# Attention's banks as two tiles, gate columns turned on VectorE and stored as rows, four pairs of modulations added in one bank each

## The chip, the cores and the metric

The kernel runs on one NeuronCore of one Trainium2 chip. The core has a matrix engine (TensorE, PE in the profile), three other compute engines (VectorE or DVE, ScalarE or ACT, GpSimd or POOL), a sync engine (SP) that issues transfers, and 16 DMA engines. Each engine runs its own queue in order and waits on semaphores of the others. TensorE writes only to PSUM, 8 banks of 512 float32 values in each of 128 partitions. The metric is the device time of one execution in microseconds (us); times before and after are compared by medians of several runs.

## What is computed

One layer of a hybrid block on 512 latent tokens with 256 context tokens, D_MODEL = 2048, all in float32. The parts that the change touches are the modulation vectors and the gate (first and last lines) and attention.

```python
shift, scale, gate = jnp.split(silu_c @ w_ada[l] + b_ada[l], 3, axis=-1)
shift_c, scale_c, gate_c = jnp.split(silu_cc @ w_ada[l] + b_ada[l], 3, axis=-1)
h = _modulate(_rmsnorm(xs, norm_g[l]), shift[:, None], scale[:, None])
hc = _modulate(_rmsnorm(cs, norm_g[l]), shift_c, scale_c)
...
p = h @ w_l
q = _rope(_rmsnorm(_heads(p, OFF_Q, N_Q_HEADS), q_norm_g[l]), cos, sin) * q_scale
...
attn = _attention(q, jnp.concatenate([k, kc], axis=1), jnp.concatenate([v, vc], axis=1))
y = _merge(p[..., OFF_ZA:], attn, w_proj_a[l], w_proj_b[l], w_out[l])
new_xs = xs + gate[:, None] * y
```

`_merge` multiplies attention and a Fourier mix with SiLU gates, projects both, weighs them with sigmoid gates and applies the output projection; the output is a final RMSNorm.

## The kernel before

Large products are made in three passes on split operands (`mm3`, lines 339 to 341): each float32 operand is split into a rounded part and its remainder (`split_from`, line 181 on ScalarE, line 182 on VectorE), and high x high, high x low and low x high are added in PSUM. Most weight products use a two by two block scheme with seven products (`Group`, P1 to Q4).

The start (to about 130 us) makes the modulations and the first projection. The columns of `x` are walked in 16 blocks of 128 channels (`KK = 16`). For one block `kb`, `modulate(kb)` takes a bank (`bank2`, tag `pd` in the profile), runs 16 matrix-vector products (`matvec`, line 567; the profile has two records for each) with the block's shift and scale weights as the moving operand, and copies the 128 x 256 result to SBUF on ScalarE (`taken`, line 583). The stationary operand is `c2`: for each of 16 row blocks, 32 columns, of which the first two hold silu of the two conditioning vectors and the rest zeros. Four row blocks run in the four column strips of the array, so the result has four groups of 32 rows, with the sums in the first two rows of each. `turned(kb)` turns the copy with two transposes (line 588) into the other half of the same bank, `factors(kb)` adds the four groups on VectorE (line 599) and makes the columns `gain` and `shift` (lines 600 and 602), and `make_h` applies them to `x`. Blocks 6 to 13 go in four pairs (the loop at line 844): both matrix-vector runs, each followed by its copy and the loads of the block two further on (line 477), some other matmuls (`some`), the transposes of both, then `factors` and `make_h` for each. In this part the orders of TensorE, ScalarE and VectorE are those of the text (`manual_schedule`); later a scheduler orders the engines by priority.

From about 150 to 803 us eight weight groups run (two-bank tiles `x` and `y` from the pool `psp`, tags x, y0 and y1). The last product of the last group sums into `x` tiles; at its end ScalarE copies one (line 1160) and VectorE reads another (line 1089). Then attention's pool `psq` is opened (line 1461): one tile `banks` of eight banks, of which the views `banks[0]` are the first six and `banks[1]` the last two. The six hold four score and transpose areas of 768 columns (`wide`); of the two, one is the accumulator of the filler (a branch projection that is interleaved with attention), the other serves values and query transposes. `reuse_waits="tile"` makes a new tile's first user wait for the users of the older tiles that lay in its place. TensorE starts attention with two filler steps of three matmuls each (line 1496), then the scores of step 0.

The gate vector is made on VectorE: 32 products with row sums (line 1369) leave two halves for each of 16 blocks in `gparts`, 128 partitions x 32 columns. After attention (lines 1744 to 1746) the halves and the bias are added into `gcol` (128 x 16), and GpSimd's queue stores it to `gs` in DRAM as 16 rows of 128, that is, turned by the access pattern of the store. `load_rows` (line 1783) reads `gs` as rows, broadcast to all partitions, about 100 us later. GpSimd's queue also issues the accumulating loads of the seven-product scheme (line 292) and the gate loads (line 1636).

Of the kernel before, what the change touches and what calls it, by code (L numbers as in the profile page):

```python
# [10 lines left out]
F32 = mybir.dt.float32  # L11
F32R = mybir.dt.float32r
ACT = mybir.ActivationFunctionType
ALU = mybir.AluOpType
AX = mybir.AxisListType
# [3 lines left out]
P = 128  # L19
# [3 lines left out]
KK = D // P  # L23
# [100 lines left out]
def block_kernel(ctx, tc, xT, ctx_rows, ctx_toks, x, c_row, w_ss, w_gate, vecs, qkg, rope, dft_c, dft_s,  # L124
                 w_start, w_g, w_pab, w_o, final_g, out):
    nc = tc.nc
# [6 lines left out]
    const = sb("const")  # L133
# [9 lines left out]
    gs = dsc.tile([KK, P], F32, name="gs")  # L143
# [13 lines left out]
    def uid(s):  # L157
        cnt[0] += 1
        return f"{s}{cnt[0]}"
# [14 lines left out]
    def bank2():  # L174
        return ps.tile([P, 512], F32, tag="b2", bufs=2, name=uid("pd"))
# [179 lines left out]
    cvt, bada, ng = small[:, : 2 * KK], small[:, 2 * KK : 5 * KK], small[:, 5 * KK :]  # L355
# [1 line left out]
    nc.vector.tensor_scalar(bsc1, bada[:, KK : 2 * KK], 1.0, None, op0=ALU.add)  # L357
    shift = const.tile([P, KK, 2], F32, name="shift")
    gain = const.tile([P, KK, 2], F32, name="gain")
    gcol = const.tile([P, KK], F32, name="gcol")  # L360
    gparts = const.tile([P, 2 * KK], F32, name="gparts")

    pairs = []
# [58 lines left out]
    for g in range(LAST + 1):  # L422
        for name in ONE_GROUP:
            if (g, name) == (LAST, "Q4"):
                stream_keys(0)
            if g == KV:
                f = CTX_FORMS.index(next(f for n, f, _, _ in PRODUCTS if n == name))
                stream(("cf", name), cf_d[:, :, f].rearrange("i p j c -> p i j c"), 1024, 8, dst=ctx_tiles)
            stream_product(name, g, w_g[g], BY_DVE_GATES if g else ())
            for pc in range(4):  # L430
                p = context_piece(g, name, pc)
# [36 lines left out]
    pa, pap = region("pa", "right")  # L468
# [16 lines left out]
    def load_start():  # L485

        may[0] = 1
        with tc.issue_after(last_load[0]):
            load_more()
        assert not may[0]  # L490
        last_load[0] = asked[0].ins

    def wada_load(kb):
        r = []
        for h in range(2):
            r.append(pap.tile([P, 8, 256], F32, tag="wada", bufs=4, name=uid("wa")))
            for k in (0, 4) if (kb, h) == (0, 1) else (0,):
                n = 4 if (kb, h) == (0, 1) else 8
                ask(nc.sync, r[-1][:, k : k + n, :], w_ss[kb, :, 8 * h + k : 8 * h + k + n, :])
        return r  # L500
# [3 lines left out]
    wada = {0: wada_load(0)}  # L504
# [2 lines left out]
    wada[1] = wada_load(1)  # L507
    load_start()

    c2 = pap.tile([P, KK, 32], F32, name="c2")  # L510
    nc.vector.memset(c2, 0.0)
    rt = pap.tile([P, 1], F32, name="rt")
    ce = pap.tile([P, 2 * KK], F32, name="ce")
    with tc.issue_after(nc.scalar.activation(ce, cvt, ACT.Exp, scale=-1.0).ins):
        nc.scalar.activation(rt, ones[:, 0:1], ACT.Sqrt)
    nc.vector.tensor_scalar(ce, ce, 1.0, None, op0=ALU.add)
    nc.vector.reciprocal(ce, ce)
    nc.vector.tensor_tensor(c2[:, :, 0:2].rearrange("p k j -> p j k"),
                            cvt.rearrange("p (j k) -> p j k", j=2),
                            ce.rearrange("p (j k) -> p j k", j=2), op=ALU.mult)  # L520
    fch = ppool.tile([P, 2, 2 * P], F32R, name="fch")
# [38 lines left out]
            nc.tensor.matmul(acc[:, t * P : t * P + P], pick[:, t, :], r, start=True, stop=True)  # L560
        return acc

    def matvec(kb, h):
        acc, w = two[kb][:, :256], wada[kb][h]
        for k in range(8):
            j, n = k % 4, 8 * h + k
            nc.tensor.matmul(acc[32 * j : 32 * j + 32], c2[:, n, :], w[:, k, :], start=n < 4, stop=n >= KK - 4)

    o_of, sp_of = {}, {}

    two = {}

    def modulate(kb, meanwhile=lambda: None):
        two[kb] = bank2()
        for h in range(2):
            matvec(kb, h)
        meanwhile()
        return taken(kb)

    def taken(kb):  # L580
        o = o_of[kb] = pap.tile([P, 256], F32, tag="ada_o", bufs=2, name=uid("ado"))
        wada.pop(kb)
        return nc.scalar.copy(o, two[kb][:, :256])

    def turned(kb):
        o = o_of.pop(kb)
        for i in range(2):
            nc.tensor.transpose(two[kb][:, 256 + P * i : 256 + P * i + P], o[:, P * i : P * i + P], ident)
        if kb == 0:
            warm(3, o)  # L590

    def columns(kb):
        turned(kb)
        factors(kb)

    def factors(kb):
        sp = two.pop(kb)[:, 256:]
        r = pap.tile([P, 2, 2], F32, tag="ada_r", bufs=2, name=uid("adr"))
        nc.vector.tensor_reduce(r, sp.rearrange("p (h g r) -> p h r g", h=2, g=4)[:, :, 0:2, :], axis=AX.X, op=ALU.add)
        nc.vector.tensor_scalar(gain[:, kb, :], r[:, 1, :], bsc1[:, kb : kb + 1], ng[:, kb : kb + 1],  # L600
                                op0=ALU.add, op1=ALU.mult)
        last = nc.vector.tensor_scalar(shift[:, kb, :], r[:, 0, :], bada[:, kb : kb + 1], None, op0=ALU.add)
        return last
# [173 lines left out]
    with tc.manual_schedule(engines={E.PE}):  # L777
        warm(8, ones)
        norms = token_norms()
        two[0] = bank2()  # L780
        matvec(0, 0)
        rx0.append(spread(*norms))
        matvec(0, 1)
        with tc.manual_schedule(engines={E.Activation, E.DVE}):
            nc.scalar.copy(rx, rx0[0])
            by_root(0)
            split_next()
            taken(0)
            wada[2] = wada_load(2)
            load_start()  # L790
            columns(0)
            row_hi(0)
            scaled(0)
            row_lo(0)
            split_next()
            by_root(1)
            some(4)
            modulate(1)
            rest = split_hi()
            wada[3] = wada_load(3)  # L800
            load_start()
            some(1)
            columns(1)
            some(1)
            row_hi(1)
            rest()
            scaled(1)
            row_lo(1)
            some(2)
            for kb in range(1, 4):  # L810
                k = kb + 1
                some(2 + (kb == 1))
                by_root(k)
                modulate(k, split_next)
                if kb < 3:
                    wada[k + 2] = wada_load(k + 2)
                    load_start()
                hold()
                some(2 - (kb == 1))
                columns(k)  # L820
                row_hi(k)
                release()
                scaled(k)
                if kb < 3:
                    some(2)
                row_lo(k)
                if kb == 3:
                    some(2)
                    by_root(5)
                    modulate(5)  # L830
                    for k in (6, 7):
                        wada[k] = wada_load(k)
                        load_start()
                    hold()
                    some(2)
                    columns(5)
                    row_hi(5)
                    release()
                    scaled(5)
                    load_rope()  # L840
                    row_lo(5)
                else:
                    some(2)
            for kb in range(4, KK - 4, 2):
                some(3)
                split_next()
                some(5)
                split_next()
                if kb == 6:
                    rotations()  # L850
                k = kb + 2
                for i in range(2):
                    modulate(k + i)
                    if k + 2 + i < KK:
                        wada[k + 2 + i] = wada_load(k + 2 + i)
                        for _ in range(2 if k + 2 + i == KK - 3 else 1):
                            load_start()
                some(1)
                for i in range(2):
                    turned(k + i)  # L860
                factors(k)
                make_h(k, lambda: some(1))
                factors(k + 1)
                make_h(k + 1, lambda: some(1))
                if k >= 8:
                    form_row(k - 8)
                    form_row(k - 7)
                some(1)
                if kb == KK - 6:
                    split_table(0)  # L870
                    split_from(get(("dftc", 0)), fch[:, 0, :], fch[:, 1, :])
                    load_start()
            for k in (KK - 2, KK - 1):
                some(2 if k < KK - 1 else 3)
                modulate(k)
                some(1)
                columns(k)
                make_h(k)
                split_next()
                if k < KK - 1:  # L880
                    load_start()
                form_row(k - 8)
        some(1)
        some(8)
# [95 lines left out]
    banks = []  # L980
# [478 lines left out]

    pgs.close()  # L1460
    psq = ctx.enter_context(tc.tile_pool(name="psq", bufs=1, space=PSUM, reuse_waits="tile"))
    whole_psum = psq.tile([P, 8, 512], F32, name="banks")
    banks += [whole_psum[:, :6, :], whole_psum[:, 6:, :]]
    last_y[:] = [0, 0]
    wide = [flat(banks[0])[:, NKEY * i : NKEY * i + NKEY] for i in range(4)]
    fill_acc, b1 = banks[1][:, 0, :], lambda: banks[1][:, 1, :]
# [219 lines left out]
    for i in range(NSTEP + 3):  # L1686
        h, t = divmod(i, 4)
# [20 lines left out]
        n = next((n for n, at in enumerate(SUM_AT) if at <= i < at + 3), None)  # L1708
# [19 lines left out]
        if i in GATE_STEPS:  # L1728
            n = NGATE + GATE_STEPS.index(i)
# [6 lines left out]
        if i == NSTEP - 1:  # L1736
            a_groups.append(a_group(0))
            first = a_groups[0].steps("P1")
# [2 lines left out]
            next(first)  # L1741
    ats_.close()
    left[3] = 0
    nc.vector.tensor_tensor(gcol, gparts[:, :KK], gparts[:, KK:], op=ALU.add)
    nc.vector.tensor_tensor(gcol, gcol, bada[:, 2 * KK :], op=ALU.add)
    nc.gpsimd.dma_start(gs.rearrange("k p -> p k"), gcol)


    gp = ctx.enter_context(tc.tile_pool(name="gp", bufs=1, side="right", reuse_waits="tile"))
# [320 lines left out]
```

## Time and profile before

| what | value |
|---|---|
| runs | 1285.94 us median of 3 (1285.69 to 1288.67) |
| profiled execution | 1286.97 us, its span 1285.2 us |
| granted TensorE clock | 0.999 |
| DMA moved | 319.07 MB, mean 248 GB/s |
| under 512 B | 9889 of 104343 packets |

A busy time counts the union of an engine's instructions. TensorE's matmuls overlap each other in the records, so the distance between the starts of two matmuls, not the length of one, says what a matmul costs in a stream. In a row of a timeline the first two numbers are the start in the span and the duration in us, and brackets hold the idle time before and what ended it. In a row of windows, the busy time of each engine follows the window's length in the order PE, weight loads (PEld), DVE, ACT, POOL, then the granted clock, the DMA engines' busy share and GB/s. A row of a line or tile has its instructions' shortest, median and longest duration in ns.

### The profile page before, as it was taken

The numbers are of one execution on the slowest core, as the hardware profiler recorded it, in microseconds if no ns is written. First come the engines' busy times: TensorE is split into PE (matmuls) and PEld (weight loads), VectorE is DVE, ScalarE is ACT, GpSimd is POOL, SyncE is SP. The second block draws the span as 40 slices with busy tenths as digits, with TensorE's granted clock in tenths as the row PEclk, the third lists the DMA queues.
The fourth block names the chain that finished last, engine by engine and source line by source line (L and its number), as shares of the span: only waits on it lengthen the run. The fifth ranks groups of instructions, "written<-read, shape, count | busy, mean of one in ns | idle before, by whom it ended". The sixth has DMA issues, their size and how long they took to land.

```text
span 1285.2 us, 17638 instructions
## 1 busy us (share of the span) xinstructions
PE 1269.6 (99%) x6562; PEld 1045.2 (81%) x6562; DVE 991.0 (77%) x1305; ACT 683.2 (53%) x1077; POOL 173.2 (13%) x226
## 2 busy tenths in 40 slices
PE   8999999999999999999999999999999999999997
PEld 5677888888888888888888888888888888888886
DVE  5767899889778787748687756778898777787677
ACT  5322765555466564543355445766667646465544
POOL 0000121111102011012021011011100221211310
PEclk9999999999999999999999999999999999999999
DMA  9998798888898998887879897578852989998986
GB/s 378 412 368 344 242 204 254 229 240 239 234 315 209 320 271 254 291 197 188 282 204 288 254 259 234 180 234 250 265 178 67 260 241 258 245 207 222 227 207 179
DMA packets 104343, 319.07 MB, mean 248 GB/s; under 512 B 9889, under 2 KB 32801, under 8 KB 100289
## 3 DMA queue, kind: packets, MB, share of 16 engines
q1 hardware_dynamic: 54336, 195.24, 41.8%
q0 software_dynamic: 27600, 100.29, 37.0%
q10 hardware_dynamic: 22320, 22.42, 5.1%
q8 instruction: 51, 0.84, 0.3%
q14 instruction: 36, 0.29, 0.1%
HBM read 283.30 MB, written 34.61 MB: 247 GB/s over the span
## 4 chain that ended last, share of the span: by engine, by line
PE 82%; DVE 3%; DMA 2%; ACT 2%; issue 1%; SPq 0%; ACTq 0%
PE banks L339 10%; PE banks L340 10%; PE banks L341 10%; PE x L341 9%; PE x L339 9%; PE x L340 9%; PE y L341 8%; PE y L340 8%; PE y L339 8%; PE banks L1551 2%; DMA wr<-in_w_pab 1%; DVE wlo L182 1%; DMA s<-yb_d 1%; PE banks L1665 1%; DVE s L182 0%
## 5 line engine op out<-in xcount | busy, mean ns | idle before, releaser
L181 ACT ACTIVATE whi<-R 128x1024 fp32r<-128x1024 f32 x138 | 145.1, 1058 | 143.7 <-PE banks L341 47.5
L182 DVE TENSOR_TENSOR wlo<-R,whi 128x1024 fp32r<-128x1024 f32 x138 | 167.7, 1221 | 61.2 <-ACT whi L181 60.9
L182 DVE TENSOR_TENSOR wlo<-wr,whi 128x1024 fp32r<-128x1024 f32 (+1 forms) x122 | 147.3, 1213 | 62.7 <-ACT whi L181 62.5
L181 ACT ACTIVATE whi<-wr 128x1024 fp32r<-128x1024 f32 (+1 forms) x122 | 127.4, 1050 | 123.4 <-PE y L341 33.0
L339 PE MATMUL banks<-whi,s 128*128 128x512 f32 (+1 forms) x400 | 157.8, 394 | 0.9 <-ACT ev L1160 0.7
L340 PE MATMUL banks<-wlo,s 128*128 128x512 f32 (+1 forms) x400 | 155.9, 390 | 0.0
L341 PE MATMUL banks<-whi,s 128*128 128x512 f32 (+1 forms) x400 | 155.8, 389 | 0.0
L339 PE MATMUL x<-whi,s 128*128 128x512 f32 x352 | 137.1, 390 | 0.0
L341 PE MATMUL x<-whi,s 128*128 128x512 f32 x352 | 137.0, 389 | 0.0
L340 PE MATMUL x<-wlo,s 128*128 128x512 f32 x352 | 136.9, 389 | 0.0
L292 POOL DMA_DIRECT2D R<-in_w_g x68 | 59.5, 874 | 484.7 <-DVE wlo L182 290.2
L340 PE MATMUL y<-wlo,s 128*128 128x512 f32 x316 | 123.0, 389 | 0.1
L339 PE MATMUL y<-whi,s 128*128 128x512 f32 x316 | 122.9, 389 | 0.0
L341 PE MATMUL y<-whi,s 128*128 128x512 f32 x316 | 122.8, 389 | 0.0
L181 ACT ACTIVATE s<-wr 128x512 fp32r<-128x512 f32 (+2 forms) x93 | 60.8, 677 | 66.0 <-DMA wr<-cf_d 24.4
L182 DVE TENSOR_TENSOR s<-wr,s 128x512 fp32r<-128x512 f32 (+2 forms) x93 | 66.7, 749 | 31.8 <-ACT s L181 30.9
L339 PEld LDWEIGHTS banks<-whi,s 128*128 128x128 f32 x400 | 75.2, 188 | 16.6 <-ACT ev L1160 1.1
L341 PEld LDWEIGHTS banks<-whi,s 128*128 128x128 f32 x400 | 75.2, 188 | 15.3
L340 PEld LDWEIGHTS banks<-wlo,s 128*128 128x128 f32 x400 | 75.2, 188 | 13.9 <-DVE wlo L182 0.2
L340 PEld LDWEIGHTS x<-wlo,s 128*128 128x128 f32 x352 | 66.1, 188 | 13.8
L341 PEld LDWEIGHTS x<-whi,s 128*128 128x128 f32 x352 | 66.1, 188 | 13.7
L339 PEld LDWEIGHTS x<-whi,s 128*128 128x128 f32 x352 | 66.1, 188 | 13.6
(333 smaller groups left out, 2794.0 us busy)
## 6 DMA issues: line engine op xcount, KB each, us to landing
wr<-in_w_g SPq DMA_DIRECT2D x124, 512.0 KB, 5.6
R<-in_w_g POOLq DMA_DIRECT2D x68, 512.0 KB, 7.4
wa<-in_w_ss SPq DMA_DIRECT2D x31, 1024.0 KB, 9.5
R<-in_w_g SPq DMA_DIRECT2D x32, 512.0 KB, 5.8
wr<-in_w_gate SPq DMA_DIRECT2D x32, 512.0 KB, 5.1
wr<-in_w_o SPq DMA_DIRECT2D x24, 512.0 KB, 7.1
R<-in_w_o POOLq DMA_DIRECT2D x24, 512.0 KB, 8.9
wr<-in_w_pab SPq DMA_DIRECT2D x20, 512.0 KB, 6.1
```

The source lines that it names most:

```text
L181: first = nc.scalar.activation(hi, src, ACT.Copy)
L182: return first, nc.vector.tensor_tensor(lo, src, hi.bitcast(F32), op=ALU.subtract)
L292: chained[:] = [nc.gpsimd.dma_start(chain[e.pc], e.nxt, accum_op=ALU.add)]
L339: nc.tensor.matmul(o, ah, bh, start=start, stop=False, skip_group_check=cont)
L340: nc.tensor.matmul(o, ah, bl, start=False, stop=False, skip_group_check=cont)
L341: nc.tensor.matmul(o, al, bh, start=False, stop=stop, skip_group_check=cont)
L1551: nc.tensor.transpose(tp[:, k * P : (k + 1) * P], p[:, k * P : (k + 1) * P], ident)
L1665: last_turn[0] = nc.tensor.transpose(tp[:, k // 2, 256 * (k % 2) + P * t : 256 * (k % 2) + P * t + P], m[:, t, k * P : k * P + P], ident)
```

## The change

Three edits. The stationary operand gets 34 columns for each row block with the two vectors in columns 2 and 3; a pair's first run takes columns 2 to 33, its second columns 0 to 31, so that its sums come to rows 2 and 3 of each group, and both runs add into one bank. One copy, two transposes and one reduction over four rows then serve both blocks. Attention's eight banks become a tile of six and a tile of two. The gate's halves are added in place, VectorE transposes the 128 x 32 tile in blocks of 32 x 32, and four stores write 16 rows of 32 values each.

```diff
-    gcol = const.tile([P, KK], F32, name="gcol")
+    gcol = const.tile([P, 2 * KK], F32, name="gcol")
...
-    c2 = pap.tile([P, KK, 32], F32, name="c2")
+    c2 = pap.tile([P, KK, 34], F32, name="c2")
     nc.vector.memset(c2, 0.0)
...
-    nc.vector.tensor_tensor(c2[:, :, 0:2].rearrange("p k j -> p j k"),
+    nc.vector.tensor_tensor(c2[:, :, 2:4].rearrange("p k j -> p j k"),
...
-    def matvec(kb, h):
-        acc, w = two[kb][:, :256], wada[kb][h]
+    def matvec(kb, h, first=True, last=True):
+        acc, w, c = two[kb][:, :256], wada[kb][h], c2[:, :, 2:34] if first else c2[:, :, 0:32]
         for k in range(8):
             j, n = k % 4, 8 * h + k
-            nc.tensor.matmul(acc[32 * j : 32 * j + 32], c2[:, n, :], w[:, k, :], start=n < 4, stop=n >= KK - 4)
+            nc.tensor.matmul(acc[32 * j : 32 * j + 32], c[:, n, :], w[:, k, :], start=first and n < 4,
+                             stop=last and n >= KK - 4, skip_group_check=not (first and last))
...
+    def modulate_pair(kb, loads):
+        two[kb] = two[kb + 1] = bank2()
+        for i in range(2):
+            for h in range(2):
+                matvec(kb + i, h, i == 0, i == 1)
+            if i:
+                taken(kb)
+            wada.pop(kb + i, None)
+            loads(kb + i)
+
     def taken(kb):
         o = o_of[kb] = pap.tile([P, 256], F32, tag="ada_o", bufs=2, name=uid("ado"))
-        wada.pop(kb)
+        wada.pop(kb, None)
         return nc.scalar.copy(o, two[kb][:, :256])
...
+    r_of = {}
+
     def factors(kb):
         sp = two.pop(kb)[:, 256:]
-        r = pap.tile([P, 2, 2], F32, tag="ada_r", bufs=2, name=uid("adr"))
-        nc.vector.tensor_reduce(r, sp.rearrange("p (h g r) -> p h r g", h=2, g=4)[:, :, 0:2, :], axis=AX.X, op=ALU.add)
+        if kb not in r_of:
+            n = 4 if kb + 1 in two else 2
+            r = pap.tile([P, 2, 4], F32, tag="ada_r", bufs=2, name=uid("adr"))
+            nc.vector.tensor_reduce(r[:, :, :n], sp.rearrange("p (h g r) -> p h r g", h=2, g=4)[:, :, 0:n, :],
+                                    axis=AX.X, op=ALU.add)
+            r_of[kb] = r[:, :, 0:2]
+            if n == 4:
+                r_of[kb + 1] = r[:, :, 2:4]
+        r = r_of.pop(kb)
...
-                for i in range(2):
-                    modulate(k + i)
-                    if k + 2 + i < KK:
-                        wada[k + 2 + i] = wada_load(k + 2 + i)
-                        for _ in range(2 if k + 2 + i == KK - 3 else 1):
-                            load_start()
+
+                def loads(k):
+                    wada[k + 2] = wada_load(k + 2)
+                    for _ in range(2 if k + 2 == KK - 3 else 1):
+                        load_start()
+
+                modulate_pair(k, loads)
                 some(1)
-                for i in range(2):
-                    turned(k + i)
+                turned(k)
                 factors(k)
...
-    whole_psum = psq.tile([P, 8, 512], F32, name="banks")
-    banks += [whole_psum[:, :6, :], whole_psum[:, 6:, :]]
+    banks += [psq.tile([P, n, 512], F32, name=f"banks{n}") for n in (6, 2)]
...
-    nc.vector.tensor_tensor(gcol, gparts[:, :KK], gparts[:, KK:], op=ALU.add)
-    nc.vector.tensor_tensor(gcol, gcol, bada[:, 2 * KK :], op=ALU.add)
-    nc.gpsimd.dma_start(gs.rearrange("k p -> p k"), gcol)
+    nc.vector.tensor_tensor(gparts[:, :KK], gparts[:, :KK], gparts[:, KK:], op=ALU.add)
+    nc.vector.tensor_tensor(gparts[:, :KK], gparts[:, :KK], bada[:, 2 * KK :], op=ALU.add)
+    nc.vector.transpose(gcol, gparts)
+    for i in range(0, P, 32):
+        nc.gpsimd.dma_start(gs[:, i : i + 32], gcol[i : i + KK, :])
```

## The prediction

> **What bounds it now.** I read the page's busy times first, then the chain that ended last, then stages, and last who keeps TensorE waiting.
>
> ```profile
> span 1285.2 us, 17638 instructions
> ...
> PE 1269.6 (99%) x6562; PEld 1045.2 (81%) x6562; DVE 991.0 (77%) x1305; ACT 683.2 (53%) x1077; POOL 173.2 (13%) x226
> ...
> PE 82%; DVE 3%; DMA 2%; ACT 2%; issue 1%; SPq 0%; ACTq 0%
> ```
>
> TensorE is busy in 99% of the span and the chain is its own; the steps below can gain only by issuing fewer matmuls or by closing the few places where TensorE waits. The stages (us of the window, then busy us of each engine) and TensorE's waits after the start say how few those are:
>
> ```profile
> 20.00:125.00 105.00, 104.10 (x814) 74.80 (x818) 70.35 (x146) 32.05 (x49) 1.81 (x3) 1.00 0.96 384
> 170.00:800.00 630.00, 630.00 (x2785) 521.44 (x2786) 486.88 (x591) 321.26 (x517) 82.34 (x94) 1.00 0.86 249
> 815.00:900.00 85.00, 83.45 (x559) 72.71 (x558) 70.18 (x114) 56.67 (x110) 14.26 (x24) 1.00 0.71 220
> ```
>
> ```profile
> PE banks L1389 <- DVE ptl L182: 0.8, 1, 0.8
> PE banks L339 <- ACT ev L1160: 0.7, 1, 0.7
> PE banks L1665 <- DMA s<-yb_d: 0.7, 1, 0.7
> ```
>
> From 170 to 800 us TensorE is never idle. The change touches three places: the modulations (62 to 114 us), the step into attention (803 us) and the gate columns (988 us).
>
> The profiled execution took 1286.97 us, 1.77 around its span; the median of the runs is 1285.94. I take differences from the profiled execution and set them against the median, since that is what is measured again.
>
> **The modulations.** A pair today issues 64 matrix-vector records, some other matmuls, and then four transposes. Before the pairs, a single modulation issues two.
>
> ```profile
> 56.72 0.39 PE L341 MATMUL pc<-s,wlo 128*128 128x512 f32 x1
> 56.95 0.38 PE L588 MATMUL pd<-ident,ado 128*128 128x128 f32 x2
> ...
> 57.40 0.40 PE L340 MATMUL pb<-wlo,s 128*128 128x512 f32 x1
> ...
> 67.57 0.39 PE L341 MATMUL pc<-s,wlo 128*128 128x512 f32 x1
> 67.80 0.60 PE L588 MATMUL pd<-ident,ado 128*128 128x128 f32 x4
> ...
> 68.47 0.40 PE L340 MATMUL pc<-s,whi 128*128 128x512 f32 x1
> ```
>
> Durations overlap, so I take starts: from the matmul before the transposes to the second one after them it is 57.40 - 56.72 = 0.68 us with two transposes and 68.47 - 67.57 = 0.90 with four. Two fewer are worth 0.22 us, and four pairs 0.88 us. The 64 records stay: the second modulation's weights only stand two columns further, so its sums land in two other rows of each group of 32. The Trainium skill ("TensorE: Matmul & The Clock Gate", Back-to-back issue gap) gives about 81 ns for a matmul of 128 columns in a stream; by that the eight would be worth an estimated 0.65 us, against 0.88 from these starts.
>
> The other engines lose four copies on ScalarE and four reductions on VectorE:
>
> ```profile
> L567 PEld LDWEIGHTS pd<-wa,c x512: 106/110/110, 16.6 to 125.7; 128*32 128x32 f32 x171
> ...
> L583 ACT COPY ado<-pd x16: 354/374/374, 20.0 to 126.4; 128x256 f32<-128x256 f32 x16
> ...
> L599 DVE TENSOR_REDUCE adr<-pd x16: 163/167/175, 20.9 to 127.7; 128x4 f32<-128x16 f32 x16
> ```
>
> That is 4 x 0.37 us and 4 x 0.17 us, in a stage where ScalarE is busy 32 of 105 us and VectorE 70: nothing for the end. The four reductions that stay give eight sums instead of four; the row's 0.17 us bounds what they grow by, and it is given back by the reduction removed. The remaining copy starts when the second half of the pair is done, as the second copy does now, and the transposes come a stretch of matmuls later, as now; no wait is added. The loads of the next weights are issued at the same two points of TensorE's order.
>
> Is that 0.88 us real, if DMA paces the stage (share 0.96, 384 GB/s)? The weight loads say how late they land:
>
> ```profile
> 95.97 1.14 SPq L477 DMA_DIRECT2D wa<-in_w_ss  x2
> ...
> 108.23 3.66 PE L567 MATMUL pd<-wa,c 128*32 128x256 f32 x64
> ...
> DMA to landing us min/median/max: 3.9/8.8/12.9
> ```
>
> The last quarter of the fourth pair's weights is issued about 96.8 us; with the longest landing, 12.9, it is there at 109.7, and it is used in the last quarter of a 3.66-us run, at about 110.9. Three pairs have then gained 0.66 us, so 1.2 us of margin becomes 0.5. It holds, with little to spare; if the loads came an extra us late the gain here would be lost again. I take 0.88, and keep 0 to 0.88.
>
> **The banks.** Attention's PSUM is one tile of eight banks now, so its first writer waits for the last reader of any tile that lay there before. With two tiles the filler's two-bank tile waits only for readers of those two banks.
>
> ```profile
> 795.39 0.69 DVE L182 TENSOR_TENSOR s<-y,s 128x512 fp32r<-128x512 f32 x1 [2.03 <-ACT s L181]
> ...
> 802.54 0.39 PE L341 MATMUL x<-whi,s 128*128 128x512 f32 x1
> ...
> 802.97 0.59 ACT L1160 COPY ev<-x 128x512 f32<-128x512 f32 x1 [1.66 <-PE x L341]
> ...
> 803.60 0.50 PE L339 MATMUL banks<-whi,s 128*128 128x512 f32 x1 [0.68 <-ACT ev L1160]
> 803.94 0.39 PE L340 MATMUL banks<-wlo,s 128*128 128x512 f32 x1
> 804.17 0.40 PE L341 MATMUL banks<-whi,s 128*128 128x512 f32 x1
> ...
> 805.10 0.28 PE L339 MATMUL banks<-s,s 128*128 128x256 f32 x1
> ```
>
> The wait is for ScalarE's copy out of an x tile. The first tiles of the pool before attention are made in the order x, y, x, y, or all x first; either way the last two banks were a y tile, whose last reader (the first row) ended at 796.08. The filler's six matmuls, first in TensorE's order, can then follow at the usual distance, 804.17 - 803.94 = 0.23 us. Saved: 803.60 - 802.54 - 0.23 = 0.83, and 803.94 - 803.60 - 0.23 = 0.11 of the restart, together 0.94 us. What is late next are the scores in the six-bank tile: six matmuls take 1.4 us, so scores come at 804.2, after the copy's end at 803.56. Behind them ScalarE takes the first exponential, behind the same work as now, so I let it stay where it is:
>
> ```profile
> 807.34 0.90 ACT L1535 ACTIVATE s<-banks,gain 128x768 f32<-128x768 f32 x1 [0.21 <-DVE gain L1533]
> ...
> 809.70 0.60 PE L1551 MATMUL banks<-ident,s 128*128 128x128 f32 x4
> ```
>
> It ends at 808.24, and TensorE, 0.94 us earlier, would ask for it at 808.76: still in time. I take 0.94, bounded by 0 (the tile lies otherwise) and 0.94.
>
> **The gate columns.** Now one store of 4-byte pieces, later two additions, a 32x32-block transpose of 32 columns and four stores of 128-byte rows.
>
> ```profile
> 988.37 0.18 DVE L1745 TENSOR_TENSOR gcol<-gcol,small 128x16 f32<-128x16 f32 x1
> ...
> 989.01 1.20 POOL L1746 DMA_DIRECT2D gs<-gcol  x1 [14.92 <-DVE gcol L1745]
> ...
> 990.00:995.00 5.00, 5.00 (x39) 4.72 (x38) 4.61 (x7) 4.64 (x9) 1.65 (x3) 1.00 0.18 2
> ...
> 991.95 0.90 POOL L292 DMA_DIRECT2D R<-in_w_pab  x1 [1.74 <-DVE wlo L182]
> ...
> 1091.87 0.55 POOL L1783 DMA_DIRECT2D s<-gs  x1 [5.30 <-DVE s L182]
> ...
> 1110.77 9.82 DMA s<-yb_d
> 1120.63 1.09 PE banks L1665 x8
> ```
>
> The windows show a hole: from 990 to 995 us all DMA together moves 2 GB/s while the 2048 pieces go out. TensorE is busy 5.00 of those 5 us, and the first wait of TensorE for a DMA after it is the 0.7 us at L1665, at 1120.6, for a transfer issued at 1110.8; so nothing is gained at the end by closing the hole. The transpose is not in the trace; between 0 and 4 x 0.18 = 0.72 us (each 32x32 block as dear as the addition of 128x16), I take 0.2, near one such addition: VectorE is close to full there (4.61 of 5), but TensorE does not wait on it in that window. Four issues cost GpSimd 4 x 0.55 = 2.2 (as the read of gs) to 4 x 1.20 = 4.8 instead of 1.20: behind them stands the accumulation at 991.95, which arrives 1.74 us after GpSimd fell idle, so the first price hides and the second delays it by about 2 us, on a sum for a weight chunk that no wait of TensorE in the rows above goes back to. The reader of gs comes 100 us later. Taken: 0. A rule of the Trainium skill speaks against the stores ("DMA: Bandwidth & Descriptors", Specifications): below 512 bytes a piece is read, modified and written, and 128 is below; no run here shows it, and with 100 us of cover the sum stays.
>
> Sum: 0.88 + 0.94 = 1.82 us. 1286.97 - 1.8 = 1285.2 on the profiled execution's scale, **1285.94 - 1.8 = 1284.1 us** on the median's.
>
> **Rivals.** *One of the two gains is missing.* Either the bank wait stays (another tile lay under the filler's banks, or the scheduler puts the scores first), or the loads keep the modulations where they were. Against the first is the y reader at 796.08, for it that the row names only the last release. Time: 1285.94 - 0.9 = 1285.0; with neither, 1285.9, the change not doing what it says.
>
> *More than the sum.* Attention's other waits depend on how VectorE and DMA fall against TensorE: 85 - 83.45 = 1.55 us idle in 815 to 900, and 0.7 at L1665, where an accumulating DMA is late. A shifted order and free DMA could take a third or all of it: 1281.9 to 1283.3. The same shift can also cost as much.
>
> *Slower: the weight column.* The condition tile gets rows of 34 instead of 32 values, so all 512 weight loads of L567 start 8 bytes further along for each k and no longer at a multiple of 128. TensorE runs 64 of them in 3.66 us (the row at 108.23), 0.057 us each, while one load lasts 0.11: they already overlap. If a load that straddles cost a share q more and the cadence followed, that is 512 x 0.057 = 29.2 us x q: with a quarter 7.3 us, 1291.4 us. It decides, above the 0.3% bound, from q = (3.9 + 1.8)/29.2 = 0.20. Against it are reads of the moving side in rows of 258 values, where three matmuls that start at the table's first value and three that start 258 values (1032 bytes) further follow each other; the change of start lies between the first row and the second:
>
> ```profile
> 145.27 0.28 PE L341 MATMUL pc<-fsq,ul 128*128 128x258 f32 x1
> 145.39 0.28 PE L339 MATMUL pc<-fsq,uh 128*128 128x258 f32 x1
> 145.51 0.28 PE L340 MATMUL pc<-fsq,uh 128*128 128x258 f32 x1
> ```
>
> All are 0.12 us apart. The weight side itself is not shown at such a start. The same page of the Trainium skill (LDWEIGHTS, loading the stationary operand) counts only columns, not where they start; its figure for 32 columns, an estimated 27 ns, is not the row's 110.
>
> **How the numbers follow.** Both gains as computed, others within half a us: 0.52. One or both missing: 0.26. More than the sum: 0.12. Weight column: 0.04. A later order that costs 1 to 7 us: 0.06. The likeliest gives 1284.1. Runs of the kernel before lay from 1285.69 to 1288.67, so the range reaches from 1282.2 (nearly all of attention's waits gone too) to 1286.9 (nothing gained and a us lost). About 0.3%, 3.9 us, is what a measurement of this kernel can tell from no change. Faster than 1282.1: 0.06, half of the third case. Slower than 1289.8: 0.06, the weight column and a third of the last case. Same: 0.88.
>
> **What would show it.** L588 with 24 records instead of 32, L583 and L599 with 12; the stretch over the transposes 0.68 us in the pairs; the first banks matmul 0.23 us after the last x matmul; POOL with four stores of gs of some 0.55 us and no stretch at 2 GB/s near 990. The forecast is wrong if L567's runs of 64 grow from 3.66 us, if the wait on L1160 stays, if TensorE waits for DMA wa in L567 between 62 and 114 us, or if attention's idle 1.55 us grows by as much as was gained.

## The result, and the profile after

The changed kernel takes **1477.35 us** (median of 6 runs, 1474.68 to 1484.18) where the kernel before took 1286.06 in the runs beside it: a ratio of 1.149, 95% interval 1.146 to 1.152. The forecast was 1284.1 us with no measurable change. The profiled execution is the slowest of the six, 1484.18 us. From its page come the span, the busy times, TensorE's busy tenths and granted clock in 40 slices of the span, and the chain that ended last:

```profile
span 1482.4 us, 17618 instructions
...
PE 1339.8 (90%) x6554; PEld 1084.8 (73%) x6554; DVE 999.6 (67%) x1302; ACT 689.0 (46%) x1073; POOL 173.8 (12%) x229
...
PE   8999999999999999999999667677777888898996
...
PEclk9999999999999999999999889888788999999998
...
PE 13%; DVE 1%; issue 1%; ACT 1%; ACTq 0%
```

The chain is followed back over 16% of the span only, so it tells nothing of attention. TensorE does eight records fewer than before (6554 against 6562) and is busy 70 us longer. Both rows of slices fall in the same place: behind the first 22 slices, that is from about 815 us, just after attention begins. Ahead of it nothing was lost. Windows of the changed kernel (length, then busy us of PE, PEld, DVE, ACT, POOL, granted clock, DMA share, GB/s) for the start, the weight groups, attention from its first to its last exponential, and the projections behind it:

```profile
20.00:125.00 105.00, 103.83 (x810) 74.03 (x814) 69.91 (x142) 30.98 (x46) 1.80 (x3) 1.00 0.97 386
170.00:800.00 630.00, 630.00 (x2787) 521.60 (x2786) 485.80 (x590) 320.43 (x517) 81.86 (x95) 1.00 0.86 249
806.00:1141.00 335.00, 244.94 (x1251) 198.47 (x1252) 170.63 (x267) 137.72 (x256) 27.62 (x46) 0.86 0.38 115
1141.00:1480.00 339.00, 295.11 (x1307) 239.39 (x1305) 218.19 (x214) 152.84 (x187) 53.54 (x66) 0.95 0.76 187
```

The same two stages of the kernel before:

```profile
807.00:995.00 188.00, 186.09 (x1245) 163.20 (x1244) 157.22 (x257) 127.24 (x250) 25.48 (x41) 1.00 0.62 194
995.00:1284.00 289.00, 282.00 (x1316) 233.72 (x1314) 222.39 (x225) 155.31 (x193) 54.76 (x68) 1.00 0.90 228
```

Read them as a balance. Attention takes 335 instead of 188 us, 147 more, with about the same number of TensorE records. Its idle time went from 188.00 - 186.09 = 1.9 us to 335.00 - 244.94 = 90.1: 88 us of the 147. The other 59 us are busy time: about as many matmuls run longer, at a mean granted clock of 0.86. By an estimate from that clock alone, 186.09 / 0.86 = 216 us, it accounts for 30 of the 59. A matmul behind a wait lasts longer too (0.50 against 0.40 us in the first two rows of the step below); what each gives was not told apart. The projections take 339 instead of 289 us, 50 more, 37 of it idle. 147 + 50 = 197 is the whole difference of the spans, 1482.4 - 1285.2.

The waits of TensorE, by line and releaser (us in total, times, longest); in the kernel before no such row behind 800 us came to more than 0.8 us in total. The changed kernel's largest:

```profile
PE banks L339 <- DVE ptl L182: 47.4, 44, 2.9
PE banks L1570 <- ACT s L1554: 23.1, 18, 2.6
PE banks L339 <- DVE s L1129: 13.8, 5, 4.8
PE banks L339 <- ACT pth L181: 11.1, 12, 1.2
PE banks L1684 <- DMA s<-yb_d: 6.0, 3, 4.9
```

The first two make a ring. The timeline of one attention step (start, duration; in brackets the idle time before and what ended it), with L1552 the scores' maximum, L1554 their exponential, L1570 the transposes of the probabilities, and L181 and L182 the two halves of `split_from` that read the transposed probabilities:

```profile
856.88 0.50 PE L339 MATMUL banks<-s,s 128*128 128x512 f32 x1 [0.74 <-DVE ptl L182]
857.22 0.40 PE L340 MATMUL banks<-s,s 128*128 128x512 f32 x1
857.46 0.39 PE L341 MATMUL banks<-s,s 128*128 128x512 f32 x1
...
858.24 0.96 DVE L1552 TENSOR_REDUCE gain<-banks 128x1 f32<-128x768 f32 x1 [0.74 <-PE banks L341]
...
859.90 0.88 ACT L1554 ACTIVATE s<-banks,gain 128x768 f32<-128x768 f32 x1
...
860.93 0.88 PE L1570 MATMUL banks<-ident,s 128*128 128x128 f32 x6 [2.03 <-ACT s L1554]
...
861.84 0.81 ACT L181 ACTIVATE pth<-banks 128x768 fp32r<-128x768 f32 x1 [0.33 <-PE banks L1570]
...
862.68 0.96 DVE L182 TENSOR_TENSOR ptl<-banks,pth 128x768 fp32r<-128x768 f32 x1 [0.49 <-ACT pth L181]
...
863.69 0.39 PE L339 MATMUL banks<-s,s 128*128 128x256 f32 x1 [0.61 <-DVE ptl L182]
...
864.52 0.63 PE L340 MATMUL banks<-s,s 128*128 128x512 f32 x1
864.94 0.63 PE L341 MATMUL banks<-s,s 128*128 128x512 f32 x1
```

From scores to scores 6.8 us pass, and all rows with brackets, that is all links but the exponential, wait for the one before. The scores at 863.69 begin with 256 columns, so they go to the second area, `wide[1]`, columns 768 to 1535, in banks 1 and 2. They wait for VectorE to finish reading `wide[3]`, columns 2304 to 3071, in banks 4 and 5. No bank is shared and no data passes; what the two areas share is the six-bank tile. The transposes at 860.93 turn the probabilities of the step before and wait for the exponential of the newest scores, which reads another area.

Theory: a wait is drawn **for the whole tile** when the tile is smaller than PSUM, and bank by bank when one tile holds all eight banks. In the programs as built, PE waits in attention's tiles for a reader of another bank of the same tile number 0 in the kernel before and 121 in the changed one. Outside them both programs have six such waits, all in one two-bank tile `y` of the weight groups (the accumulator of line 1252, whose two banks are written in turn). Rivals: the modulations or the gate rows cost the time; or the split shifts the scheduler's order, and the order costs it; or the lower clock is the cause of the waits and not their result.

### The profile page after: what moved, and what is told of

It is laid out like the page before. It is cut to its first block, busy times and chain, and to the rows that moved or that the text cites. A ratio compares the mean times of both kernels' runs of the same rounds, so it can differ in the third digit from the quotient of the medians.

```text
span 1482.4 us, 17618 instructions
## 1 busy us (share of the span) xinstructions
PE 1339.8 (90%) x6554; PEld 1084.8 (73%) x6554; DVE 999.6 (67%) x1302; ACT 689.0 (46%) x1073; POOL 173.8 (12%) x229
## 5 line engine op out<-in xcount | busy, mean ns | idle before, releaser
L182 DVE TENSOR_TENSOR wlo<-R,whi 128x1024 fp32r<-128x1024 f32 x138 | 167.8, 1222 | 76.0 <-ACT whi L181 75.9
L181 ACT ACTIVATE whi<-R 128x1024 fp32r<-128x1024 f32 x138 | 145.2, 1058 | 156.5 <-PE banks L341 78.7
L182 DVE TENSOR_TENSOR wlo<-wr,whi 128x1024 fp32r<-128x1024 f32 (+1 forms) x122 | 147.4, 1214 | 93.0 <-ACT whi L181 92.8
L181 ACT ACTIVATE whi<-wr 128x1024 fp32r<-128x1024 f32 (+1 forms) x122 | 127.2, 1050 | 156.8 <-PE banks L341 56.1
L339 PE MATMUL banks<-whi,s 128*128 128x512 f32 (+1 forms) x400 | 167.0, 417 | 32.5 <-DVE s L1129 13.8
L340 PE MATMUL banks<-wlo,s 128*128 128x512 f32 (+1 forms) x400 | 162.0, 405 | 0.0
L341 PE MATMUL banks<-whi,s 128*128 128x512 f32 (+1 forms) x400 | 161.6, 404 | 0.0
L339 PE MATMUL x<-whi,s 128*128 128x512 f32 x352 | 137.3, 390 | 0.0
L339 PE MATMUL y<-whi,s 128*128 128x512 f32 x316 | 123.1, 390 | 0.0
L339 PEld LDWEIGHTS banks<-whi,s 128*128 128x128 f32 x400 | 79.4, 198 | 57.1 <-ACT whi L181 13.2
L339 PE MATMUL banks<-s,s 128*128 128x512 f32 (+1 forms) x160 | 67.1, 419 | 44.5 <-DVE ptl L182 44.5
L1554 ACT ACTIVATE s<-banks,gain 128x768 f32<-128x768 f32 x48 | 43.2, 900 | 126.5 <-DVE gain L1552 122.9
L181 ACT ACTIVATE s<-wr 128x512 fp32r<-128x512 f32 (+2 forms) x93 | 60.6, 677 | 69.8 <-DMA wr<-cf_d 23.3
L341 PEld LDWEIGHTS banks<-whi,s 128*128 128x128 f32 x400 | 79.2, 198 | 17.6
L182 DVE TENSOR_TENSOR ptl<-banks,pth 128x768 fp32r<-128x768 f32 x48 | 46.0, 957 | 67.6 <-ACT pth L181 67.6
L182 DVE TENSOR_TENSOR s<-wr,s 128x512 fp32r<-128x512 f32 (+2 forms) x93 | 67.0, 751 | 35.8 <-ACT s L181 32.9
L340 PEld LDWEIGHTS banks<-wlo,s 128*128 128x128 f32 x400 | 79.7, 199 | 14.7
```

The source lines that it names most:

```text
L181: first = nc.scalar.activation(hi, src, ACT.Copy)
L182: return first, nc.vector.tensor_tensor(lo, src, hi.bitcast(F32), op=ALU.subtract)
L339: nc.tensor.matmul(o, ah, bh, start=start, stop=False, skip_group_check=cont)
L340: nc.tensor.matmul(o, ah, bl, start=False, stop=False, skip_group_check=cont)
L341: nc.tensor.matmul(o, al, bh, start=False, stop=stop, skip_group_check=cont)
L1554: maxima[1] = nc.scalar.activation(probs[i], sc[:, :NKEY], ACT.Exp, bias=mx[:, 0:1], accum_out=mx[:, 1:2])
```

## The experiments

**one_tile: the changed kernel with the one tile back.**

```diff
-    banks += [psq.tile([P, n, 512], F32, name=f"banks{n}") for n in (6, 2)]
+    whole_psum = psq.tile([P, 8, 512], F32, name="banks")
+    banks += [whole_psum[:, :6, :], whole_psum[:, 6:, :]]
```

> The changed kernel with attention's banks again one tile of eight; the added modulations and the gate rows stay. If the two tiles are the cause (each matmul into a tile waits for readers of any part of it), all of the loss goes: 1284.2 to 1286.0 us, 0.9 us under before if each of the eight transposes taken out saves its 0.11 us twice as the prediction had it, nothing under before if another wait takes that up. If the modulations or the gate rows cost the time, it stays at 1470 us or more.

Measured: 1285.62 us, ratio 0.9997 (0.9988 to 1.0006). The loss is gone, and what is left of the change cannot be told from nothing.

**tiles_alone: the kernel before with the two tiles alone** (the same lines the other way round).

> The kernel before with the two tiles alone. If the two tiles are the cause: 1474 to 1482 us, with a granted clock of about 0.96 and the same waits of PE as in the changed kernel (about 47 us on L182's split of the turned probabilities). If it takes the modulations or gate rows beside them: 1286 us. If the three edits share the loss: between.

Measured: 1479.89 us, ratio 1.152 (1.148 to 1.155). Its largest wait, in the same view as above, is the changed kernel's:

```profile
PE banks L339 <- DVE ptl L182: 46.9, 44, 2.9
```

The tiles are necessary for the loss and enough for it. The modulations and the gate rows are out.

**four_tiles and two_areas: the same places, tracked differently.** Both give the scores two areas instead of three, each area two banks of its own, the transposes two banks and the filler and the values the last two. Only the tiles differ.

```diff
...
-    banks += [psq.tile([P, n, 512], F32, name=f"banks{n}") for n in (6, 2)]
+    banks += [psq.tile([P, 2, 512], F32, name=f"banks{n}") for n in range(4)]
...
-    wide = [flat(banks[0])[:, NKEY * i : NKEY * i + NKEY] for i in range(4)]
-    fill_acc, b1 = banks[1][:, 0, :], lambda: banks[1][:, 1, :]
+    wide = [flat(banks[i])[:, :NKEY] for i in (0, 1, 0, 2)]
+    fill_acc, b1 = banks[3][:, 0, :], lambda: banks[3][:, 1, :]
...
-        return wide[turn_wide[0] % 3]
+        return wide[turn_wide[0] % 2]
```

The lines left out give the pairs of the projections the same four places and split all scores after 512 columns. two_areas has instead of the first added line:

```diff
+    whole_psum = psq.tile([P, 8, 512], F32, name="banks")
+    banks += [whole_psum[:, 2 * n : 2 * n + 2, :] for n in range(4)]
```

> The changed kernel with four tiles of two banks each: scores take turns in the first two (two areas where there were three), the turned probabilities have the third, the branch's accumulator and the values the fourth. The program as built then has 40 PE waits for readers of another bank of the same tile, all in the tiles of two banks, against 121 in the changed kernel. If waits by whole tile are the cause, most of the loss goes although there are more tiles than before: 1295 to 1350 us, and the stall at a score's first matmul on L182's split of the turned probabilities is gone. If splitting the banks costs time by itself (a shifted order, placement), it stays at 1450 us or more.

> As four_tiles, with the same places in one tile of eight banks: no PE wait of the built program is for a reader of another bank. If waits by whole tile are the cause: 1284 to 1300 us, what is over 1286 being the price of two score areas for three; the difference to four_tiles is what the sharing within tiles of two banks costs. If places and order matter more than the waits, it is at four_tiles' time.

Measured: four_tiles 1297.93 us, ratio 1.009 (1.008 to 1.011); two_areas 1284.21 us, ratio 0.9987 (0.9978 to 0.9996). Twice as many tiles as in the changed kernel, and 179 of its 191 us are gone: it isn't splitting that costs, but what lies together in one tile. The windows of four_tiles for attention and the projections:

```profile
807.00:1001.00 194.00, 187.77 (x1251) 166.46 (x1251) 159.08 (x262) 130.41 (x255) 26.05 (x44) 1.00 0.60 189
1001.00:1295.00 294.00, 280.69 (x1307) 233.01 (x1305) 219.39 (x219) 153.76 (x188) 54.98 (x69) 0.99 0.88 222
```

The projections, which write pairs of banks in turn, need 294 us here and 339 with three pairs in one tile. The 13.7 us between the two kernels are the sharing that is left inside tiles of two banks. That two score areas cost nothing against three had been open: two_areas is the fastest of all, and its interval (0.9978 to 0.9996) just excludes the time of the kernel before. Why it is 1.4 us faster than one_tile (its areas share no bank with a neighbour any more) was not tried apart.

**wait_scores, wait_turns, wait_both: the waits without the tiles.** To tell waits from order and places, one_tile got the two waits of the ring written in by hand.

```diff
+    def also_waits(n, ins):
+        for i in tc.nc.cur_bb.bb.instructions[n:]:
+            tc.add_manual_dep(i, ins.name, mybir.DependencyInfo(mybir.DependencyClass.Sync, mybir.DependencyReason.DATA),
+                              reason="also waits")
...
+        n = len(tc.nc.cur_bb.bb.instructions)
         for a, b in ((0, m), (m, NKEY)):
             mm3(sc[:, a:b], qh, ql, kh[:, a:b], kl[:, a:b], True, True)
+        if last_pt[0]:
+            also_waits(n, last_pt[0].ins)
...
+        n = len(tc.nc.cur_bb.bb.instructions)
         for k in range(KT):
             nc.tensor.transpose(tp[:, k * P : (k + 1) * P], p[:, k * P : (k + 1) * P], ident)
+        also_waits(n, maxima[1].ins)
```

`last_pt` is VectorE's half of the last split, `maxima[1]` the last exponential. wait_scores has the call behind the scores, wait_turns the one behind the transposes, wait_both both.

> One tile of eight banks (as one_tile, 1285.6 us) with one wait written in beside the layer's own: all six matmuls of a score tile wait for VectorE's split of the last turned probabilities (L182 out of wide[3]); no bank is shared with it. If the waits themselves are the cause and not the tiles' places or the order, this one, which stood for 47.4 us in the changed kernel's trace, costs alone 35 to 90 us (its stalls and the clock that falls with them): 1320 to 1375 us. If other work moves into the gap once only this wait is there, under 1300 us. If tiles or places matter and waits do not: 1286 us.

> As wait_scores with the other wait alone: the six transposes of the probabilities wait for ScalarE's exp of the scores issued last (23.1 us in the changed kernel's trace). Waits as the cause: 1295 to 1330 us. Waits not the cause: 1286 us.

> Both waits in the one tile of eight banks; 76 PE waits of the built program are then for readers of another bank (121 in the changed kernel). Waits as the cause: 1360 to 1440 us, more than the two costs added, as each wait takes away the work that filled the other's gap; what is left to 1477 us is the sharing in the pairs of the filler, the values and the projections. If the waits add up simply: the sum of the two costs. Waits not the cause: 1286 us.

Measured: wait_scores 1334.47 us (ratio 1.037, 1.036 to 1.039), wait_turns 1290.24 us (1.003, 1.002 to 1.004), wait_both 1425.48 us (1.108, 1.106 to 1.109). The second wait alone costs 4 us, under the 9 to 44 that were expected (1295 to 1330 us); the first costs 48; both together 139, far more than the 52 of their sum. I read it so: with one wait alone, scores or transposes can still run ahead of the other; with both the ring is closed. The windows of wait_both:

```profile
807.00:1135.00 328.00, 242.91 (x1251) 199.01 (x1250) 168.71 (x267) 136.87 (x255) 27.56 (x46) 0.83 0.38 117
1135.00:1424.00 289.00, 281.20 (x1311) 233.31 (x1309) 216.87 (x216) 152.54 (x187) 53.50 (x66) 1.00 0.87 220
```

Attention is at 328 of the changed kernel's 335 us, with nearly the same idle time (85 us against 90) and a clock as low. The projections, where nothing was added, are back at 289. So two waits in one tile of eight banks make nearly all of attention's loss, and the tiles' places are out. The order of the engines does change with each of these kernels, as it follows from the waits; a foreign order without the waits was not tried. That wait_turns costs 4 us, with a changed order of its own, speaks against a changed order as such.

**scores_twice, scores_thrice, control_twice: is the clock cause or result?** The first issues the six matmuls of every score tile of wait_both once more ahead of the waiting six; they write the same values.

```diff
+        for _ in range(1):
+            for a, b in ((0, m), (m, NKEY)):
+                mm3(sc[:, a:b], qh, ql, kh[:, a:b], kl[:, a:b], True, True)
         n = len(tc.nc.cur_bb.bb.instructions)
         for a, b in ((0, m), (m, NKEY)):
```

scores_thrice has `range(2)`; control_twice issues the scores twice in one_tile, without added waits.

> wait_both (1425 us: attention from the first to the last exp 328 us, granted clock 0.83) with the six matmuls of every score tile issued once more ahead of those that wait, without the wait of their own; they write the same values. 48 times six matmuls, about 1.04 us each time at full clock, are 50 us more work for PE, put where it stands idle (85 us in attention). If the clock falls because PE stands idle, the clock comes back above 0.95 and the kernel gets faster although it does more: 1375 to 1410 us. If the clock falls for another reason, and the work only fills idle time: 1420 to 1435 us. If it fills nothing: 1460 to 1480 us.

> As scores_twice with two copies ahead of the waiting six, 100 us more work for 85 us of idle time. Clock follows idle time: clock at 0.99 or more in attention, but the copies no longer fit into the gaps: 1390 to 1430 us, attention near 286 us of work and what is left of idle time. Clock falls for another reason: 1450 us or more.

> one_tile (1285.6 us, no waits added) with the six matmuls of every score tile issued twice, to price the copy: PE has no idle time there, so 48 times 1.04 us come on top: 1330 to 1340 us.

Measured: scores_twice 1410.20 us, scores_thrice 1409.80 us, control_twice 1335.06 us. The control gives the copy's price, 49 us. Put into the idle time of wait_both, the same 49 us of work make the kernel 15 us **faster** (just outside the 1375 to 1410 us that were expected), and a second helping costs nothing. Attention's window of scores_twice:

```profile
807.00:1124.00 317.00, 267.50 (x1571) 219.18 (x1571) 172.36 (x271) 141.10 (x261) 27.56 (x46) 0.96 0.41 124
```

And of scores_thrice:

```profile
807.00:1120.00 313.00, 301.25 (x1832) 251.47 (x1831) 171.56 (x269) 139.04 (x256) 27.58 (x46) 0.99 0.41 123
```

The clock climbs from 0.83 to 0.96 and 0.99 as the idle time shrinks from 85 to 49.5 and 11.8 us. So the clock fell because TensorE waited. The 15 us are the least that the low clock cost, since the copies take time of their own; but at a clock of 0.96 attention still takes 317 us, 49.5 of them idle, so most of the loss is the ring's. The second helping hardly lowers the time: TensorE then has only 11.8 us left idle, and the ring's other links (maximum, exponential, copy, split) do not run on it; which of the two keeps attention at 313 us, where some 286 were expected, was not tried apart.

**mods_alone: the kernel before with the modulations' part alone.**

> The kernel before with the modulations' part alone (four pairs into one bank each, eight transposes fewer). The prediction's term: 0.9 us less, 1285.2 us; if the time goes to a later wait: 1286 us. The trace is to show the first matmul into attention's banks 0.9 us earlier.

Measured: 1285.98 us, ratio 0.9996 (0.9988 to 1.0005), which cannot tell 0.9 us from nothing. The traces can, between two fixed places: the first pair's run and the first matmul on the Fourier table behind the modulations. Before:

```profile
62.71 3.66 PE L567 MATMUL pd<-wa,c 128*32 128x256 f32 x64
...
144.30 0.28 PE L339 MATMUL pd<-fsq,uh 128*128 128x258 f32 x1
```

mods_alone:

```profile
63.22 3.66 PE L567 MATMUL pd<-wa,c 128*32 128x256 f32 x64
...
144.00 0.28 PE L339 MATMUL pd<-fsq,uh 128*128 128x258 f32 x1
```

81.59 us became 80.78: 0.81 us. The other traces agree: 81.57 in tiles_alone, which lacks the modulations' part, and 80.72 to 80.86 in those that have it, but for four_tiles with 81.33. The sign that had been named for this run, the first matmul into attention's banks 0.9 us earlier, is there by a third only:

```profile
803.29 0.50 PE L339 MATMUL banks<-whi,s 128*128 128x512 f32 x1 [0.68 <-ACT ev L1180]
```

That is 0.31 us before the 803.60 of the kernel before, as the first pair itself began 0.51 us later (63.22 against 62.71). Other traces with the part have its start at 62.81 to 63.62, tiles_alone at 62.87; why it moves was not tried.

## Why the prediction was wrong

Its small terms were right as far as the traces can tell, and the step that failed is in "The banks".

The **modulations** gave 0.81 of the predicted 0.88 us in their own stretch; whether it reaches the end is below what the times of one_tile and mods_alone can tell. The stretch over the transposes of a pair in the changed kernel is 68.73 - 68.05 = 0.68 us as forecast, and the runs of L567 still take 3.66 us, so the rival of the weight column falls, with a share q of 0:

```profile
68.05 0.40 PE L341 MATMUL pc<-s,wlo 128*128 128x512 f32 x1
68.28 0.38 PE L599 MATMUL pd<-ident,ado 128*128 128x128 f32 x2
...
68.73 0.39 PE L340 MATMUL pc<-s,whi 128*128 128x512 f32 x1
...
108.16 3.66 PE L567 MATMUL pd<-wa,c 128*32 128x256 f32 x64
```

The **step into attention** went as forecast. The filler's first matmul follows the last x matmul after 801.90 - 801.68 = 0.22 us (0.23 forecast), and the wait on L1160's copy (L1180 now) is gone:

```profile
801.68 0.39 PE L341 MATMUL x<-whi,s 128*128 128x512 f32 x1
801.90 0.39 PE L339 MATMUL banks<-whi,s 128*128 128x512 f32 x1
```

With the one tile back, in one_tile, the distance is 1.07 us again:

```profile
802.05 0.39 PE L341 MATMUL x<-whi,s 128*128 128x512 f32 x1
803.12 0.50 PE L339 MATMUL banks<-whi,s 128*128 128x512 f32 x1 [0.68 <-ACT ev L1180]
```

At the filler's first matmul the changed kernel's trace stands 803.60 - 801.90 = 1.70 us ahead, near the sum of both terms. That it fits so well is in part luck: the last x matmul alone lies between 801.59 and 802.80 in the traces with the same modulations, and at 804.73 in scores_twice.

The **gate columns** cost nothing and won nothing that the times show, as taken: in one_tile the block transpose took 0.21 us (0.2 taken) and the four stores 0.49 us each (0.55 taken), and from 990 to 995 us all DMA moves 91 GB/s where it moved 2.

```profile
987.15 0.21 DVE L1766 STREAM_TRANSPOSE gcol<-gparts 128x32 f32<-128x32 f32 x1
987.65 1.95 POOL L1768 DMA_DIRECT2D gs<-gcol  x4 [14.99 <-DVE gcol L1766]
...
990.00:995.00 5.00, 5.00 (x34) 4.48 (x33) 4.60 (x8) 4.64 (x9) 1.60 (x3) 1.00 0.61 91
```

**What failed** is the bound of the banks' term, "bounded by 0 (the tile lies otherwise) and 0.94", drawn from the sentence "With two tiles the filler's two-bank tile waits only for readers of those two banks". The sentence is true of a tile's first writer, and the step asked about nothing else. What the two tiles do to the waits inside them it put at nothing, without a reason: it took for granted that these stay as they were, bank by bank. They do not. A wait holds for the whole tile, in the six banks (attention and the pairs of the projections) and in the two, and with the two tiles alone the kernel lost 194 us (tiles_alone).

The trace of the kernel before could not show this: its tile of eight is the one whose waits go by bank, and the six waits in the two-bank tile `y` lie within 170 to 800 us, where TensorE is never idle. Its program as built could, by the count. The cost of such waits could have been worked out from rows of before: a score step took 188/47 = 4.0 us because three areas ran side by side, and the links in a row (scores 1.4 us, maximum 0.95, exponential 0.90, six transposes some 0.9, the two splits 0.81 and 0.96) come to some 6 us. The changed kernel's step is 334/47 = 7.1 us.

The rival nearest to it, "A later order that costs 1 to 7 us", had the sign, but neither the mechanism nor the size (at most 7 of 191 us), and the test named for it, attention's idle 1.55 us from 815 to 900, was the right place to look: in the same window it became 85.00 - 59.11 = 25.89 us.

```profile
815.00:900.00 85.00, 59.11 (x310) 48.60 (x308) 41.10 (x63) 33.90 (x63) 7.46 (x12) 0.86 0.38 112
```

The Trainium skill ("TensorE: Matmul & The Clock Gate", HAM oscillation — how this bites in real kernels) asks for no idle gap of TensorE above about 3.4 us. That rule would have passed attention, whose longest wait is the 2.9 us at L339 (those of 4.8 and 4.9 lie in the projections), and yet its mean clock is 0.86: here the measurement decides. The page's next section (A second HAM failure mode: psum-queue depth-cycling) names frequent short gaps between groups of matmuls as another way to a clock that swings. With that the trace agrees: within one step, matmuls of 512 columns start 0.24 us apart at 857 and 0.42 us apart at 865.

## What to carry to other kernels

Before a PSUM (or any shared) tile is cut, ask by what unit the layer draws its waits for the new tiles, and count in the built program the waits whose two sides share neither data nor bank; here that count in attention's tiles went from 0 to 121. It tells where to look and not what it costs: 40 such waits in four_tiles cost 12 us, 76 in wait_both 139. What runs side by side must lie in different tiles, or in one tile that is tracked by bank; that was the tile of all eight banks, and of smaller ones only those of six and two were tried. And price two added waits together: each alone cost 48 and 4 us, both 139, and the likely reason is that only both close the ring.

## What the runs showed of the hardware

The granted clock of TensorE is not a given of the stage: short waits, none above 2.9 us, took its mean to 0.83 to 0.86 in attention. In the ring's rows a matmul of 512 columns starts 0.24 us after the one before it at 857, and 0.42 us after it at 865. Of the 59 us by which TensorE's busy time grew in the changed kernel's attention, the lower clock is an estimated 30 (186.09 / 0.86 = 216 us). In wait_both, useless matmuls in the gaps took the clock from 0.83 to 0.96 and made the kernel 15 us faster. What exactly sets the clock, the length of a gap or the share of idle time, these runs do not tell.
